# Output products of the two mixers: half of the columns by seven products for three of eight row pairs

## The chip, the cores and the metric

The kernel runs on one core of a Trainium2 chip. The core has a matrix engine (TensorE, PE in the profile, with its weight loads listed as PEld), a vector engine (DVE), a scalar engine (ACT), GpSimd (POOL) and a queue engine that issues most transfers (SP). The metric is the device time of one execution in microseconds; lower is better. All numbers are those of one core.

## The reference

Two layers over 256 tokens of width 2048, in float32. Each layer normalises, mixes tokens, adds, normalises, runs a SwiGLU feed-forward net (FFN) of width 5632, and adds. Layer 0 mixes with an mLSTM, layer 1 with an RG-LRU. Both mixers end in a product with a 2048 by 2048 matrix, and this is where the change lies:

```python
h = h + mlstm_mixer(rms_norm(h, norm_mix[0]), ...)     # ends in  (h_tilde * sigmoid(o)) @ m_w_out
h = h + swiglu(rms_norm(h, norm_ffn[0]), ...)
h = h + rglru_mixer(rms_norm(h, norm_mix[1]), ...)     # ends in  (gelu(gate) * scan) @ r_w_out
h = h + swiglu(rms_norm(h, norm_ffn[1]), ...)
out = rms_norm(h, norm_final)
```

## The kernel before

Weights are read once, in tiles of two 128-row blocks by 512 columns (`raw`, 512 KB each). Every float32 factor is split into a high part, rounded to the PE's reduced type (`whi`, a cast on ACT), and the rest (`wlo`, a subtraction on DVE), and a product is three matmuls: high by high, high by low, low by high. The activations are the stationary operand, in blocks of 128 rows by 128 tokens; the weights move, 512 columns at a time. One accumulator fills one of the eight PSUM banks.

Two routines make products with tokens in the rows. `linear_tok` takes one group of 512 columns (a "quarter" of 2048) and goes through the 16 row blocks k, with two accumulators (the two blocks of 128 tokens). Its weights come through `stream`, whose casts and splits are given a high priority, so that a scheduler, which sets each engine's order when the program is built, puts them ahead of other work. `project_out` calls it once per quarter, adds the result to the residual `h`, and puts the next norm's transposes for that quarter into a list (`later`) that is worked off between matmul groups (`run_pending`).

`paired` takes two groups of 512 columns at once and goes through the row blocks two by two, so that a "row pair" is a 2 by 2 block product: two row blocks by two column groups, for two token blocks. A plain row pair takes eight block products of three matmuls. A row pair that is listed in `seven` takes seven, by Winograd's form of Strassen's scheme: from the four weight tiles of 128 by 512 it makes four differences in place, in the two `raw` tiles, and splits them into four tiles, called s, u, v and t in the code (s, v and t hold 1024 columns, u 512), and the stationary operands include four sums and differences of activation blocks ("forms", s1 to s4). The products go into banks 1 to 8 in the order s, s, u, v, v, t, t; after the last seven pair `mid` adds up banks 1, 5, 6 and 7 (`sums`) so that four banks are free again. Splits in `paired` have no raised priority. The FFN uses it for all of its products.

The tiles `raw`, `whi` and `wlo` come from pools of four buffers, handed out as they are released. The FFN's own pool lends two more of each:

```python
if more[0] and turns[tag] % 6 > 3:
    return more[0].tile([P, 2, NB], dt, tag=tag, name=name, bufs=2)
return wpool.tile([P, 2, NB], dt, tag=tag, name=name)
```

In the mixers `more[0]` is empty, and there are four.

In the mLSTM, four steps j each compute v and o with `linear_tok`, then `turn_y` transposes the gated output `y` and splits it into two of the 16 row blocks (`yh`, `yl`). In the RG-LRU, `gates`, `gelu_branch` and `combine` make a group of four row blocks (`zh`, `zl`); the last group's GELU product (`gb`) is the last PE work before the output product `po`.

Of the kernel before, what the change touches and what calls it, by code (L numbers as in the profile page):

```python
# [38 lines left out]
def kernel(  # L39
# [426 lines left out]


# [14 lines left out]
    def mlstm_mixer():  # L482
        with tc.tile_pool(name="mx", bufs=2) as mx:
# [149 lines left out]
            def turn_y(j, i, y, hi, lo):  # L633
                pt = misc(f"ty{j}{i}").rearrange("p (f t) -> p f t", f=2)
                for f in range(2):
                    for b in range(NT):
                        nc.tensor.transpose(
                            pt[:, f, b * P:(b + 1) * P], y[:, b, (2 * i + f) * P:(2 * i + f + 1) * P], ident
                        )
                for f in range(2):  # L640
                    g = par["g_head"][:, 4 * j + 2 * i + f:4 * j + 2 * i + f + 1]
                    nc.scalar.activation(hi[:, 2 * i + f, :], pt[:, f, :], AF.Copy, scale=g)
# [39 lines left out]
    def ffn(layer, n, nxt):  # L682
        with tc.tile_pool(name=f"ff{layer}", bufs=1) as fp:
            more[0] = fp
            turns.update(raw=-1, whi=-1, wlo=-1)
# [3 lines left out]
            part = {}  # L689

            def sums(bank):

                ea = fp.tile([P, 2, NB], F32, tag="ea", name="ea")
                eb = fp.tile([P, 2, NB], F32, tag="eb", name="eb")
                nc.scalar.copy(ea[:, 0, :], bank[1])
                nc.vector.tensor_tensor(ea[:, 1, :], bank[6], ea[:, 0, :], op=ALU.add)
                nc.vector.tensor_tensor(eb[:, 0, :], bank[7], ea[:, 1, :], op=ALU.add)
                nc.vector.tensor_tensor(ea[:, 1, :], bank[5], ea[:, 1, :], op=ALU.add)
                nc.vector.tensor_tensor(eb[:, 1, :], bank[5], eb[:, 0, :], op=ALU.add)
                part["e"] = ea, eb  # L700

# [32 lines left out]

            def add_out(q, wc, np_, seven, form, last=None):
                def mid(bank):
                    sums(bank)
                    for b, e in enumerate(part["e"]):
                        hs = h[:, b, q * NB:(q + 2) * NB]
                        nc.vector.tensor_tensor(hs, hs, e.rearrange("p s n -> p (s n)"), op=ALU.add)  # L740

                if last:
                    order = [p for p in range(np_) if p not in (np_ - 3, np_ - 1)] + [np_ - 3, np_ - 1]
                    bank = paired(wc, (q * NB, (q + 1) * NB), np_, seven, form, f"po{q}", mid, order, 2)
                    for b, i in enumerate(((2, 3), (4, 8))):
                        last.store(b, [bank[k] for k in i])
                    return
                bank = paired(wc, (q * NB, (q + 1) * NB), np_, seven, form, f"po{q}", mid)
                for i, b, s in ((2, 0, 0), (4, 1, 0), (3, 0, 1), (8, 1, 1)):
                    hs = h[:, b, (q + s) * NB:(q + s + 1) * NB]  # L750
                    nc.vector.tensor_tensor(hs, bank[i], hs, op=ALU.add)
# [47 lines left out]
    def rglru_mixer():  # L799
        with tc.tile_pool(name="rg", bufs=1) as rg:  # L800
# [80 lines left out]
            def combine(j):  # L881
                ge, hs = ges[j], hss[j]
                nc.vector.tensor_tensor(ge, ge, hs, op=ALU.mult)
# [94 lines left out]
```

## Time and profile before

| | us |
|---|---|
| median of three runs (2095.2 to 2096.41) | 2096.27 |
| the profiled execution | 2097.5 |
| its span, first to last instruction | 2095.7 |
| PE busy, DVE busy, ACT busy | 2079.8, 1782.5, 1186.8 |
| mLSTM's output product on PE, first to last matmul's start | 308.4 to 398.9 |
| RG-LRU's output product on PE | 1299.2 to 1388.7 |

In the tables, `out<-in` are the program's names for what an instruction writes and reads; `p` are the FFN's first products and `po` all output products. Idle time is that before an instruction, with what ended it. Busy PE time is modelled, since matmuls overlap; the step from one matmul's start to the next is what counts. Line numbers in the profile are those of the kernel before; the changed kernel's are two higher in the helpers (L447 becomes L449), and further off behind them.

### The profile page before, as it was taken

To read this page: it belongs to the slowest core of one execution; us is meant where nothing else is said; L and a number is where in the kernel's file an instruction comes from. 1 tells how busy PE (TensorE), PEld (TensorE's weight loads), DVE (VectorE), ACT (ScalarE), POOL (GpSimd) and SP (SyncE) were. 2 spreads that over 40 slices of the span, in tenths; PEclk is the share of its full clock that TensorE was granted. 3 is DMA by queue.
4 is the path that set the end of the run, shared out by engine and by line. 5 is a ranking of instruction groups with operands and counts; after the bars stand their busy time and mean duration, and the time that the engine had idled before them with its cause. 6 is when DMAs were issued, how large, how long until landed. Compare 5 with 4: busy or idle time off the path is not lost.

```text
span 2095.7 us, 27022 instructions
## 1 busy us (share of the span) xinstructions
PE 2079.8 (99%) x9794; PEld 1736.4 (83%) x9794; DVE 1782.5 (85%) x2260; ACT 1186.8 (57%) x1529; POOL 40.6 (2%) x60
## 2 busy tenths in 40 slices
PE   9999999999999999999999999999999999999997
PEld 7888888888888888888888888888888888888886
DVE  6755555699999999999997888679999999999998
ACT  5444445556565555565656778556555555555554
POOL 0011110000000000000000000000000000000010
PEclk9999999999999999999999999999999999999999
DMA  7556666666555666665656666666655666656564
GB/s 216 171 161 181 181 181 181 197 205 209 194 201 183 206 213 201 198 203 199 197 189 172 190 190 184 190 200 194 219 183 189 201 205 202 205 197 224 191 201 141
DMA packets 211375, 405.73 MB, mean 194 GB/s; under 512 B 14552, under 2 KB 14760, under 8 KB 211112
## 3 DMA queue, kind: packets, MB, share of 16 engines
q1 hardware_dynamic: 210520, 401.89, 60.0%
q10 hardware_dynamic: 720, 2.10, 0.3%
q8 instruction: 77, 1.26, 0.2%
q14 instruction: 58, 0.48, 0.1%
HBM read 401.84 MB, written 2.10 MB: 193 GB/s over the span
## 4 chain that ended last, share of the span: by engine, by line
PE 96%; DVE 2%; DMA 1%; issue 1%; ACT 0%; POOL 0%; POOLq 0%; SPq 0%; ACTq 0%; DVEq 0%
PE p L384 15%; PE p L386 15%; PE p L385 15%; PE po L385 7%; PE po L386 7%; PE po L384 7%; PE gb L231 3%; PE rec L231 3%; PE po L207 3%; PE po L206 3%; PE po L205 3%; PE qk L231 2%; PE gb L234 1%; PE rec L234 1%; PE v L205 1%; PE v L207 1%
## 5 line engine op out<-in xcount | busy, mean ns | idle before, releaser
L446 ACT CAST whi<-raw 128x1024 fp32r<-128x1024 f32 (+1 forms) x732 | 689.8, 991 | 590.3 <-DVE raw L399 346.0
L447 DVE TENSOR_TENSOR wlo<-raw,whi 128x1024 fp32r<-128x1024 f32 (+1 forms) x732 | 807.8, 1150 | 72.2 <-ACT whi L446 68.8
L384 PE MATMUL p<-whi,z_f 128*128 128x512 f32 x1342 | 523.9, 390 | 0.0
L386 PE MATMUL p<-whi,z_f 128*128 128x512 f32 x1342 | 522.2, 389 | 0.0
L385 PE MATMUL p<-wlo,z_f 128*128 128x512 f32 x1342 | 522.2, 389 | 0.0
L177 DVE TENSOR_TENSOR wlo<-raw,whi 128x1024 fp32r<-128x1024 f32 (+1 forms) x225 | 273.6, 1218 | 172.9 <-ACT whi L175 172.7
L175 ACT CAST whi<-raw 128x1024 fp32r<-128x1024 f32 (+1 forms) x225 | 235.6, 1049 | 209.8 <-PE po L207 64.4
L386 PEld LDWEIGHTS p<-whi,z_f 128*128 128x128 f32 x1342 | 251.9, 188 | 52.5
L384 PEld LDWEIGHTS p<-whi,z_f 128*128 128x128 f32 x1342 | 251.9, 188 | 52.1 <-DVE h L447 0.5
L385 PEld LDWEIGHTS p<-wlo,z_f 128*128 128x128 f32 x1342 | 252.0, 188 | 51.6
L385 PE MATMUL po<-wlo,h 128*128 128x512 f32 x668 | 260.5, 390 | 1.6 <-DVE wlo L447 1.6
L386 PE MATMUL po<-whi,h 128*128 128x512 f32 x668 | 260.0, 389 | 0.0
L384 PE MATMUL po<-whi,h 128*128 128x512 f32 x668 | 259.3, 390 | 0.0
L385 PEld LDWEIGHTS po<-wlo,h 128*128 128x128 f32 x668 | 125.4, 188 | 29.2 <-DVE wlo L447 3.5
L386 PEld LDWEIGHTS po<-whi,h 128*128 128x128 f32 x668 | 125.4, 188 | 25.9
L384 PEld LDWEIGHTS po<-whi,h 128*128 128x128 f32 x668 | 125.3, 188 | 26.0 <-ACT whi L446 0.2
L231 PE MATMUL qk<-x_m,whi 128*128 128x512 f32 x256 | 81.1, 399 | 0.0
L231 PE MATMUL rec<-x_m,whi 128*128 128x512 f32 x256 | 80.5, 396 | 0.0
L231 PE MATMUL gb<-x_m,whi 128*128 128x512 f32 x256 | 80.4, 395 | 0.0
L399 DVE TENSOR_TENSOR raw<-raw,raw 128x512 f32<-128x512 f32 x102 | 70.6, 692 | 3.4
L401 DVE TENSOR_TENSOR raw<-raw,raw 128x512 f32<-128x512 f32 x102 | 70.6, 692 | 3.4
L398 DVE TENSOR_TENSOR raw<-raw 128x512 f32<-128x512 f32 x102 | 70.5, 691 | 3.3
(255 smaller groups left out, 2470.8 us busy)
## 6 DMA issues: line engine op xcount, KB each, us to landing
raw<-in_ffn_w_in_dram SPq DMA_DIRECT2D x352, 512.0 KB, 4.8
raw<-in_ffn_w_out_dram SPq DMA_DIRECT2D x176, 512.0 KB, 5.4
raw<-in_m_w_in_dram SPq DMA_DIRECT2D x95, 512.0 KB, 3.7
raw<-in_r_w_in_dram SPq DMA_DIRECT2D x64, 512.0 KB, 3.9
raw<-in_m_w_out_dram SPq DMA_DIRECT2D x32, 512.0 KB, 3.7
raw<-in_r_w_out_dram SPq DMA_DIRECT2D x32, 512.0 KB, 4.2
gr<-in_r_gate_w_dram SPq DMA_DIRECT2D x8, 512.0 KB, 3.6
h<-in_x_dram SPq DMA_DIRECT2D x4, 512.0 KB, 8.0
```

The costliest lines, as they stand in the source:

```text
L175: cast = nc.scalar.copy(hi[:, at, 0:ncols], r)
L177: nc.vector.tensor_tensor(lo[:, at, 0:ncols], r, hi[:, at, 0:ncols].bitcast(F32), op=ALU.subtract)
L205: nc.tensor.matmul(o, lhsT=ah[:, bs], rhs=hi, start=(k == 0), stop=False)
L207: nc.tensor.matmul(o, lhsT=al[:, bs], rhs=hi, start=False, stop=(k == nk - 1))
L231: nc.tensor.matmul(ps[f], lhsT=hi[:, f * P:(f + 1) * P], rhs=act2(k), start=(k == 0), stop=False, skip_group_check=True)
L384: nc.tensor.matmul(o, lhsT=ah, rhs=bh, start=i not in begun, stop=False)
L385: nc.tensor.matmul(o, lhsT=ah, rhs=bl, start=False, stop=False)
L386: nc.tensor.matmul(o, lhsT=al, rhs=bh, start=False, stop=stop and p == end[i])
L399: nc.vector.tensor_tensor(rb[:, 1, :], rb[:, 1, :], ra[:, 0, :], op=ALU.add)
L401: nc.vector.tensor_tensor(ra[:, 1, :], ra[:, 1, :], rb[:, 1, :], op=ALU.subtract)
L446: nc.scalar.copy(dst_hi, src)
L447: nc.vector.tensor_tensor(dst_lo, src, dst_hi.bitcast(F32), op=ALU.subtract)
```

## The change

In both mixers the first two quarters become one `paired` call over eight row pairs, with seven products in pairs 2, 4 and 6; quarters 2 and 3 go through `project_out` as before. The forms for these three pairs are made where the mixer's output is split. `sums` and `add_out` move out of the FFN unchanged.

```diff
+SEVEN_M = (2, 4, 6)
+SEVEN_R = (2, 4, 6)
...
+    def mixer_out(w, ys, ss, seven, nxt):
+        def form(p, name):
+            if name[0] == "s":
+                return tuple(v[:, int(name[1]) - 1, :] for v in ss[p])
+            f, b = 2 * (p % 2) + int(name[2]) - 1, int(name[1]) - 1
+            return tuple(v[:, f, b * P:(b + 1) * P] for v in ys[p // 2])
+
+        add_out(0, w, NK // 2, seven, form)
+        for q in range(2):
+            later(lambda q=q: nxt.done(q), 4.0)
+        project_out(w, NK, lambda k: tuple(v[:, k % 4, :] for v in ys[k // 4]), nxt, (2, 3))
+
+    def mixer_forms(t, s):
+        f = scratch["forms"]()
+        for o, a, b, neg in ((0, t[1], t[3], True), (1, f[:, 0, :], t[0], True), (2, t[0], t[1], False),
+                             (3, t[2], f[:, 1, :], False)):
+            if neg:
+                nc.vector.scalar_tensor_tensor(out=f[:, o, :], in0=a, scalar=-1.0, in1=b, op0=ALU.mult, op1=ALU.subtract)
+            else:
+                nc.vector.tensor_tensor(f[:, o, :], a, b, op=ALU.subtract)
+        split_store(s[:, 0], s[:, 1], f)
+        return s[:, 0], s[:, 1]
...
@@ turn_y
+                if 2 * j + i in SEVEN_M:
+                    t = scratch["get"]().rearrange("p (s t) -> p s t", t=P)
+                    for f in range(2):
+                        nc.scalar.activation(
+                            t[:, 2 * f:2 * f + 2, :].rearrange("p s t -> p (s t)"), pt[:, f, :], AF.Copy, scale=gs[f]
+                        )
+                    split_store(*(v[:, 2 * i:2 * i + 2, :].rearrange("p f (b t) -> p (f b) t", t=P) for v in (hi, lo)),
+                                t[:, 0:4, :])
...
+                    ss[2 * j + i] = mixer_forms([t[:, n, :] for n in range(4)], sm[-1][:, at % 2])
+                    return
...
@@ mlstm_mixer
-            project_out(m_w_out[0], NK, lambda k: (yh[k // 4][:, k % 4, :], yl[k // 4][:, k % 4, :]), n1)
+            mixer_out(m_w_out[0], ys, ss, SEVEN_M, n1)
...
@@ combine
-                split_store(hi, lo, ge)
+                split_store(*ys[j], ge)
+                for i in range(2):
+                    if 2 * j + i in SEVEN_R:
+                        scratch["forms"] = lambda: rg.tile([P, 4, P], F32, tag="a2", name="forms")
+                        ss[2 * j + i] = mixer_forms(
+                            [ge[:, 2 * i + n // 2, n % 2 * P:(n % 2 + 1) * P] for n in range(4)],
+                            rg.tile([P, 2, 4, P], F32R, tag="rc" if len(ss) < 2 else "hs", name="ss", bufs=2),
+                        )
...
@@ rglru_mixer
-            project_out(r_w_out[0], NK, lambda k: (yh[k // 4][:, k % 4, :], yl[k // 4][:, k % 4, :]), n3)
+            mixer_out(r_w_out[0], ys, ss, SEVEN_R, n3)
```

What this does to the engines' orders is seen at two places; the rest of the program stands as it did. First, DVE at the start of the RG-LRU's output product. Before, the gathers of the last GELU product (L242), its norm factor (L877), its product with the scan (L883) and the split into `zl` (L447) stand between splits of weights (`wlo`, L177):

```order
L242 TENSOR_TENSOR ge_11302<-gb_2_11124,ge_11302 128x256
L177 TENSOR_TENSOR wlo_11411<-raw_11408,whi_11410 128x1024
L242 TENSOR_TENSOR ge_11302<-gb_3_11125,ge_11302 128x256
L877 TENSOR_TENSOR ge_11302<-ge_11302,rbc_m_9364 128x1024
L177 TENSOR_TENSOR wlo_11429<-raw_11426,whi_11428 128x1024
L883 TENSOR_TENSOR ge_11302<-ge_11302,hs_11117 128x1024
L177 TENSOR_TENSOR wlo_11447<-raw_11444,whi_11446 128x1024
L447 TENSOR_TENSOR zl_9257<-ge_11302,zh_9256 128x1024
L177 TENSOR_TENSOR wlo_11469<-raw_11466,whi_11468 128x1024
```

Now, from pair 2's second difference (L400) to its third and fourth splits (`wlo_11487` and `wlo_11489`, from L449), the product with the scan (L927), pair 6's forms (L519, L521) and `zl` come in between:

```order
L927 TENSOR_TENSOR ge_11380<-ge_11380,hs_11195 128x1024
L401 TENSOR_TENSOR raw_11480<-raw_11480,raw_11478 128x512
L519 SCALAR_TENSOR_TENSOR forms<-ge_11380 128x128
L521 TENSOR_TENSOR forms<-ge_11380 128x128
L519 SCALAR_TENSOR_TENSOR forms<-forms,ge_11380 128x128
L449 TENSOR_TENSOR zl_9319<-ge_11380,zh_9318 128x1024
L521 TENSOR_TENSOR forms<-ge_11380,forms 128x128
L449 TENSOR_TENSOR wlo_11487<-raw_11480,whi_11486 128x1024
L449 TENSOR_TENSOR ss<-forms,ss 128x512
L403 TENSOR_TENSOR raw_11478<-raw_11478,raw_11480 128x512
L449 TENSOR_TENSOR wlo_11489<-raw_11478,whi_11488 128x1024
```

The last group's gate and GELU work, which stood among splits of later rows, now stands ahead of two splits of row pair 2.

Second, DVE at the first addition into `h` in the mLSTM's output product. Before, a quarter's two additions (L440) stand among splits, and the norm's transposes follow a quarter later on PE:

```order
L177 TENSOR_TENSOR wlo_2850<-raw_2847,whi_2849 128x1024
L177 TENSOR_TENSOR wlo_2891<-raw_2888,whi_2890 128x1024
L440 TENSOR_TENSOR h<-po_0_2661,h 128x512
L440 TENSOR_TENSOR h<-po_1_2662,h 128x512
L177 TENSOR_TENSOR wlo_2909<-raw_2906,whi_2908 128x1024
```

Now the sums of banks 5, 6 and 7 (`e`), the additions of these sums (L487) and those of banks 2, 4, 3 and 8 (L498) come, with the splits of quarter 2 between them:

```order
L179 TENSOR_TENSOR wlo_3129<-raw_3126,whi_3128 128x1024
L478 TENSOR_TENSOR e<-po_5_2820,e 128x512
L487 TENSOR_TENSOR h<-h,e 128x1024
L179 TENSOR_TENSOR wlo_3147<-raw_3144,whi_3146 128x1024
L487 TENSOR_TENSOR h<-h,e 128x1024
L179 TENSOR_TENSOR wlo_3165<-raw_3162,whi_3164 128x1024
L498 TENSOR_TENSOR h<-po_2_2684,h 128x512
L498 TENSOR_TENSOR h<-po_4_2691,h 128x512
L498 TENSOR_TENSOR h<-po_3_2702,h 128x512
L179 TENSOR_TENSOR wlo_3183<-raw_3180,whi_3182 128x1024
L498 TENSOR_TENSOR h<-po_8_2709,h 128x512
```

Both quarters of `h` become complete together, and on PE their transposes (`tr_f`) stand within the third pair of quarter 2's row blocks:

```order
L207 MATMUL po_1_3038<-whi_3128,yh_170 128x512
L208 MATMUL po_1_3038<-wlo_3129,yh_170 128x512
L344 MATMUL tr_f_3070<-ident,h 128x128 x3
L344 MATMUL tr_f_3079<-ident,h 128x128 x3
L344 MATMUL tr_f_3099<-ident,h 128x128
L344 MATMUL tr_f_3113<-ident,h 128x128
L209 MATMUL po_1_3038<-whi_3128,yl_171 128x512
```

More of the change, by code (lines that the diff above doesn't have):

```diff
@@ L465, in log1p_exp_nabs_half, with sums, add_out, mid @@
         return p
+    part = {}
+    def sums(bank):
+        ea, eb = scratch["sums"]()
+        nc.scalar.copy(ea[:, 0, :], bank[1])
+        nc.vector.tensor_tensor(ea[:, 1, :], bank[6], ea[:, 0, :], op=ALU.add)
+        nc.vector.tensor_tensor(eb[:, 0, :], bank[7], ea[:, 1, :], op=ALU.add)
+        nc.vector.tensor_tensor(ea[:, 1, :], bank[5], ea[:, 1, :], op=ALU.add)
+        nc.vector.tensor_tensor(eb[:, 1, :], bank[5], eb[:, 0, :], op=ALU.add)
+        part["e"] = ea, eb
+    def add_out(q, w, n, seven, form, last=None):
+        def mid(bank):
+            sums(bank)
+            for b, e in enumerate(part["e"]):
+                hs = h[:, b, q * NB:(q + 2) * NB]
+                nc.vector.tensor_tensor(hs, hs, e.rearrange("p s n -> p (s n)"), op=ALU.add)
+        if last:
+            order = [p for p in range(n) if p not in (n - 3, n - 1)] + [n - 3, n - 1]
+            bank = paired(w, (q * NB, (q + 1) * NB), n, seven, form, f"po{q}", mid, order, 2)
+            for b, i in enumerate(((2, 3), (4, 8))):
+                last.store(b, [bank[k] for k in i])
+            return
+        bank = paired(w, (q * NB, (q + 1) * NB), n, seven, form, f"po{q}", mid)
+        for i, b, s in ((2, 0, 0), (4, 1, 0), (3, 0, 1), (8, 1, 1)):
+            hs = h[:, b, (q + s) * NB:(q + s + 1) * NB]
+            nc.vector.tensor_tensor(hs, bank[i], hs, op=ALU.add)
@@ L639, in turn_y @@
                         )
+                gs = [par["g_head"][:, 4 * j + 2 * i + f:4 * j + 2 * i + f + 1] for f in range(2)]
+                if 2 * j + i in SEVEN_M:
[6 more added lines that the diff above has]
+                                t[:, 0:4, :])
+                    scratch["forms"] = lambda: t[:, 4:8, :]
+                    at = len(ss)
+                    if at % 2 == 0:
+                        sm.append(mx.tile([P, 2 - at // 2, 2, 4, P], F32R, tag=("kT", "prs0")[at // 2], name="ss", bufs=1))
+                    ss[2 * j + i] = mixer_forms([t[:, n, :] for n in range(4)], sm[-1][:, at % 2])
+                    return
                 for f in range(2):
-                    g = par["g_head"][:, 4 * j + 2 * i + f:4 * j + 2 * i + f + 1]
-                    nc.scalar.activation(hi[:, 2 * i + f, :], pt[:, f, :], AF.Copy, scale=g)
+                    nc.scalar.activation(hi[:, 2 * i + f, :], pt[:, f, :], AF.Copy, scale=gs[f])
                 for f in range(2):
-                    g = par["g_head"][:, 4 * j + 2 * i + f:4 * j + 2 * i + f + 1]
                     nc.vector.scalar_tensor_tensor(
-                        out=lo[:, 2 * i + f, :], in0=pt[:, f, :], scalar=g,
+                        out=lo[:, 2 * i + f, :], in0=pt[:, f, :], scalar=gs[f],
                         in1=hi[:, 2 * i + f, :].bitcast(F32), op0=ALU.mult, op1=ALU.subtract,
                     )
-            yh, yl = [], []
+            ss, sm = {}, []
             for j in range(4):
@@ L672, in mlstm_mixer, with two @@
                 hi, lo = ys[j]
-                yh.append(hi)
-                yl.append(lo)
                 for i in range(2):
                     later(lambda i=i, y=y, hi=hi, lo=lo, j=j: turn_y(j, i, y, hi, lo))
-            project_out(m_w_out[0], NK, lambda k: (yh[k // 4][:, k % 4, :], yl[k // 4][:, k % 4, :]), n1)
+            def two():
+                e = mx.tile([P, 2, 2, NB], F32, tag="qT", name="e", bufs=1)
+                return e[:, 0], e[:, 1]
+            scratch["sums"] = two
+            mixer_out(m_w_out[0], ys, ss, SEVEN_M, n1)
     mlstm_mixer()
@@ L684, in ffn @@
             more[0] = fp
+            scratch["sums"] = lambda: [fp.tile([P, 2, NB], F32, tag=t, name=t) for t in ("ea", "eb")]
             turns.update(raw=-1, whi=-1, wlo=-1)
@@ L688, in ffn @@
             made = []
[L689 to L700, printed above, removed]
             def turn(j, i, hid, e):
@@ L733, in group @@
                 later(lambda: [turn(j, i, hid, (ea, eb)) for i in range(2)], 8.0)
[L735 to L751, printed above, removed]
             for c0, c1 in CHUNKS:
@@ L805, in rglru_mixer @@
             gwv = r_gate_w[0].rearrange("g (k p) o -> p (g k) o", p=P)
-            yh, yl = {}, {}
+            ss = {}
             rvs, rvhs, rvls, ges, hss = {}, {}, {}, {}, {}
@@ L896, in rglru_mixer @@
                     recurrent(j + 2)
-            project_out(r_w_out[0], NK, lambda k: (yh[k // 4][:, k % 4, :], yl[k // 4][:, k % 4, :]), n3)
+            scratch["sums"] = lambda: [rg.tile([P, 2, NB], F32, tag="rvh", name="e", bufs=2) for _ in range(2)]
+            mixer_out(r_w_out[0], ys, ss, SEVEN_R, n3)
     rglru_mixer()
```

3 lines of the change are left out of this document (removed).

## The prediction

> **What bounds the kernel.** I read the page first (busy times and chain), then PE's waits, then a table of stretches.
>
> ```profile
> span 2095.7 us, 27022 instructions
> PE 2079.8 (99%) x9794; PEld 1736.4 (83%) x9794; DVE 1782.5 (85%) x2260; ACT 1186.8 (57%) x1529; POOL 40.6 (2%) x60
> ...
> PE 96%; DVE 2%; DMA 1%; issue 1%; ACT 0%; POOL 0%; POOLq 0%; SPq 0%; ACTq 0%; DVEq 0%
> ```
> ```profile
> PE po L385 <- DVE wlo L447: 1.6, 2, 0.8
> ```
> ```profile
> 0.00:50.00 50.00, 45.45 (x261) 37.97 (x262) 31.68 (x68) 30.28 (x60) 3.06 (x13) 1.00 0.73 224
> ...
> 300.00:350.00 50.00, 50.00 (x230) 41.50 (x229) 27.09 (x31) 24.77 (x32) 0.00 (x0) 1.00 0.62 186
> ...
> 500.00:550.00 50.00, 50.00 (x226) 41.51 (x225) 47.53 (x59) 28.38 (x34) 0.00 (x0) 1.00 0.54 180
> ...
> 1250.00:1300.00 50.00, 50.00 (x303) 44.32 (x302) 40.08 (x49) 45.88 (x65) 0.00 (x0) 1.00 0.63 190
> ...
> 2050.00:2100.00 50.00, 35.75 (x156) 28.62 (x154) 37.40 (x53) 21.20 (x33) 1.10 (x2) 0.93 0.36 126
> ```
>
> PE is the bound from end to end: 96% of the chain, and in all FFN and mixer products only 1.6 us of waiting. So a matmul that goes saves its whole interval, and any wait that comes is paid in full. The columns of the table after the stretch and its length are busy PE, PE loads, DVE, ACT, POOL, then clock, DMA share and GB/s. The mLSTM output products (300 to 350) leave DVE 23 us idle of 50; the FFN, which already uses seven products, leaves it 2.5.
>
> **Term A, the matmuls.** First and last of 46 matmuls in a row of the RG-LRU output product:
>
> ```profile
> 1299.18 0.40 PE L205 MATMUL po<-whi,zh 128*128 128x512 f32 x1
> ...
> 1309.39 0.39 PE L205 MATMUL po<-whi,zh 128*128 128x512 f32 x1
> ```
>
> 10.21 us over 45 steps is 0.227 us each. A row pair of 512 by 512 weights costs 24 matmuls (5.45 us) plain and 21 (4.77 us) with seven products. Three pairs in two mixers save 18 matmuls: **4.1 us**, which is 0.195%. That is all there is to win.
>
> **What is added.** Per mixer, forms of three activation pairs (four 128-wide operations, a 512-wide cast and a 512-wide low half each) and, per seven pair, a third 1024-wide split, a 512-wide one and four 512-wide differences where two 1024-wide splits stood.
>
> ```profile
> L447 DVE TENSOR_TENSOR wlo<-raw,whi 128x1024 fp32r<-128x1024 f32 x630 | 743.5, 1224 | 72.2 <-ACT whi L446 68.8
> L446 ACT CAST whi<-raw 128x1024 fp32r<-128x1024 f32 x630 | 634.3, 1052 | 578.7 <-DVE raw L399 346.0 <-PE p L386 89.5 <-PE po L386 60.2
> ...
> L399 DVE TENSOR_TENSOR raw<-raw,raw 128x512 f32<-128x512 f32 x102 | 70.6, 692 | 3.4
> ...
> L446 ACT CAST whi<-raw 128x512 fp32r<-128x512 f32 x102 | 62.7, 615 | 11.6 <-PE po L386 9.9 <-ACT whi L446 1.6
> ...
> L330 DVE TENSOR_TENSOR zh<-zh 128x128 f32<-128x128 f32 x36 | 10.2, 284 | 0.0
> ...
> L642 ACT ACTIVATE yh<-ty,cols 128x256 fp32r<-128x256 f32 x16 | 6.7, 469 | 3.2 <-PE ty L637 3.2
> ```
> DVE, then ACT, in the FFN's output product, where this path runs today:
> ```profile
> 714.51 1.22 DVE L740 TENSOR_TENSOR h<-h,ea 128x1024 f32<-128x1024 f32 x1
> 715.64 1.22 DVE L740 TENSOR_TENSOR h<-h,eb 128x1024 f32<-128x1024 f32 x1
> 716.78 2.48 DVE L751 TENSOR_TENSOR h<-po,h 128x512 f32<-128x512 f32 x4
> ...
> 722.04 0.68 DVE L397 TENSOR_TENSOR raw<-raw,raw 128x512 f32<-128x512 f32 x1
> 722.76 0.69 DVE L398 TENSOR_TENSOR raw<-raw 128x512 f32<-128x512 f32 x1
> 723.49 0.69 DVE L399 TENSOR_TENSOR raw<-raw,raw 128x512 f32<-128x512 f32 x1
> ```
> ```profile
> 724.50 3.90 ACT L446 CAST whi<-raw 128x1024 fp32r<-128x1024 f32 x4 [7.54 <-PE po L386]
> ```
>
> Back to back, DVE starts a 1024-wide operation every 1.13 us and a 512-wide one every 0.60 (2.48 less 0.68, over 3); where one needs the one before it, 0.72. ACT starts the cast 0.3 us after DVE's third difference ends (723.49 + 0.69 to 724.50). A seven pair thus takes DVE 3 x 1.13 + 0.60 + 4 x 0.72 = 6.9 us where a plain one takes 2.3, in 4.77 us of PE. Forms for pairs 2 and 4 are made while v, o and gb products run; I cost them at nothing, under DVE's 23 idle us, though ACT at 1250 to 1300 has only 4 us left, so the 512-wide cast (0.6 us) may push what follows there. The transposes of y, the norm's transposes and the DMA count stay as they were.
>
> **Term B, the RG-LRU mixer's entry.** Gate arithmetic and GELU of the last quarter come on DVE when po begins at 1299.18. Today they end late and harm nobody, since weight splits go ahead of them and their result is needed by k = 12 only:
>
> ```profile
> 1296.55 1.06 ACT L865 ACTIVATE th<-th 128x1024 f32<-128x1024 f32 x1
> ```
> ```profile
> 1297.64 1.23 DVE L866 SCALAR_TENSOR_TENSOR th<-th,ii 128x1024 f32<-128x1024 f32 x1 [0.95 <-ACT th L865]
> ...
> 1302.19 1.27 DVE L870 TENSOR_TENSOR_SCAN hs<-r,th 128x256 f32<-128x256 f32 x2
> ...
> 1305.68 1.06 DVE L242 TENSOR_TENSOR ge<-gb,ge 128x256 f32<-128x256 f32 x3
> ...
> 1311.02 1.23 DVE L883 TENSOR_TENSOR ge<-ge,hs 128x1024 f32<-128x1024 f32 x1 [0.42 <-ACT ge L878]
> ```
>
> In the new order they, and the forms of pair 6, stand on DVE ahead of pair 2's third and fourth splits. From L866 (waiting for the root on ACT, so no earlier) to pair 2's last low half I count ten 1024-wide operations (11.3), four scans at 0.6 (2.4), four gathers (1.06 for three: 1.4), six 512-wide at 0.6 to 0.72 (4.0), four forms (1.1): 20.2 us without a pause. One pause is sure: the last cast waits for the last difference (0.3 + 1.05 us), with nothing else queued. So the split is done 20.2 + 1.4 us after 1297.64, that is 20.0 us after po begins. PE wants it after two plain pairs and 18 matmuls, 10.9 + 4.1 = 15.0 us. **Wait 5.1 us**, in pieces under 2 us (first for the third split's cast, then its low half, then the fourth's). Bounds: 3.7 without the pause, 5.7 with ACT 0.6 us late.
>
> **Term C, raw buffers.** The FFN's pools lend two more buffers of each kind; the mixers have four, and a row pair takes two raw ones. So pair 4 loads into pair 2's two, pair 6 into pair 4's, and these are free only when DVE has made the last splits. Landing of the mixers' loads, mLSTM's and RG-LRU's:
>
> ```profile
> DMA to landing us min/median/max: 3.6/4.0/6.2
> ```
> ```profile
> DMA to landing us min/median/max: 3.5/4.3/6.7
> ```
>
> One turn from third split to third split: issue 0.1, landing 4.0, cast 1.05, splits 1.13 + 0.6, three differences 2.16, hand-over 0.3, cast 1.05, split 1.22: 11.6 us. PE's turn is 5.45 + 4.77 = 10.2, so each turn loses 1.4 us once slack is gone. In the mLSTM mixer pair 2's third split is ready about 2 us before its matmul (transposes of y after pair 0 at 5.5 us, then ACT's two 0.47 and two 0.6, the third split's 1.05 + 1.22, and about 2 us for transposes, hand-overs and the buffer that pair 1 frees: 11.8, wanted at 13.9), so pair 4 is covered and pair 6 waits about 1.0. In RG-LRU pair 2 is late already; pairs 4 and 6 wait 1.1 each. **3.2 us**; with landings of 3.6 about 0.5, with 6.2 to 6.7 about 10. I take the medians, since pair 4's two loads are let go 1.1 us apart (third split, then fourth) and DMA is at 0.62 of its time in this stage.
>
> **Term D, the exit.** The norm's transposes of quarters 0 and 1 stand on PE 27 (mLSTM) and 32 matmuls into quarter 2 and need all of h's additions. On DVE, from pair 6's last split to the first finished block of h, stand seven 1024-wide splits (7.9), four sums (2.6), two 1024-wide additions (2.4) and one 512-wide (0.6): 13.5 us, plus a wait of up to 1 us for a buffer that PE frees late. PE arrives after 56 or 61 matmuls, 12.7 or 13.8 us, and the last block of h follows one split and three additions later. I take 1.2 + 0.8 = **2.0 us**; 0 to 4 as the buffer wait falls. Queued behind PE's wait are quarter 2's matmuls, so it is paid. Quarter 2's first two loads go past nothing new on SP, but use pair 6's raw buffers: free some 8 us before PE needs their splits, against 4.0 for landing and 2.3 for a split, so I cost them at nothing; landing at 6.5, they would cost about 0.7. POOL's moved memset is under its 98% of idle time.
>
> **Sum.** -4.1 + 5.1 + 3.2 + 2.0 = +6.2 us. The profiled execution took 2097.5 us (span 2095.7), 1.2 above the median 2096.27: profiled span near 2102, median **2102.5 us**. All low ends give 2096.4, all high ends 2112.
>
> **Rivals.**
> (1) Not slower. Averages decide: a mixer's added DVE work is 3 x 4.6 + 3 x 1.9 = 19.5 us against 40 idle us in its 90 us of output products. That needs pair 2's last split within 15.0 us of po's start, so DVE would have to reach the chain at 1297.64 some 5 us earlier; ACT's root there speaks against it. Time 2092.2, or 2094 with half of D.
> (2) Only the entry waits: landings near 3.6 and a free buffer at the exit hide C and D: 2096.27 - 4.1 + 5.1 = 2097.3.
> (3) Loads land late, near 6.5 us, because pairs of them leave together: C rises to 10, time 2109.
> (4) The waits slow PE's clock. After the last matmul the clock falls: 0.93 over the 45.7 us that are left in the last stretch is some 6.4 us at half. One such stretch within the mixer costs 3.2 us: 2105.7; two, 2109. Against it: PE waited 4.5 us in its first 50 and the clock there is 1.00. The Trainium skill (TensorE: Matmul & The Clock Gate, Part 1) says that the clock halves after an idle window of about 3.4 us; by that rule gaps under 2 us between matmuls cost nothing more, and the trace agrees as far as it goes.
>
> **Chances.** The forecast (2099.5 to 2105.5) 0.52, (1) 0.15, (2) 0.13, (3) 0.12, (4) 0.08. What a measurement of this kernel can tell from no change is about 0.2%, 4.2 us. Term A alone stays within that, so faster has 0.02; (1), (2) and the lower end of the forecast make 0.29 for the same; slower 0.69. The range leaves out (1) and the upper ends of (3) and (4): 2096.5 to 2109.
>
> **What would show it.** PE's waits should name L387 and L386 of po on wlo and whi, about 10 us in all, the largest part within 25 us of RG-LRU's po. DVE should be busy without a pause there. The norm's transposes should wait for h once or twice per mixer. PE's matmuls must be 18 fewer. If PE shows no wait on po, B is wrong and (1) holds; if the mLSTM mixer waits more than RG-LRU, C is mis-sized.

## Result, and the profile after

The changed kernel takes 2106.39 us (median of four, 2103.69 to 2108.98) against 2095.87 for the kernel before (median of four): a ratio of 1.0048, 95% interval 1.0036 to 1.006, or 10.5 us slower. The profiled execution took 2103.69 us, the lowest of the four.

From the page, span and busy times:

```profile
span 2101.9 us, 27100 instructions
PE 2080.4 (99%) x9776; PEld 1734.0 (82%) x9776; DVE 1824.4 (87%) x2335; ACT 1198.8 (57%) x1552; POOL 40.6 (2%) x60
```

PE has 18 matmuls fewer (9794 before), and DVE 41.9 us more work. From the table of waits, PE's own on `po` and `tr_f` (total us, how often, the longest):

```profile
PE po L387 <- DVE wlo L449: 3.5, 5, 0.9
PE po L386 <- ACT whi L448: 3.0, 4, 1.3
PE tr_f L344 <- DVE h L498: 2.9, 2, 2.0
```

Two of the five waits in the first row, 1.6 us together, stand in the FFN and were there before. The mixers have thus 1.9 + 3.0 + 2.9 = 7.8 us of new waits. Their places are in PE's timeline (start, length, then in brackets the idle time before the instruction and what ended it); the first two lines are from the mLSTM's output product, the others from the RG-LRU's, which begins at 1298.82:

```profile
342.26 0.50 PE L387 MATMUL po<-wlo,ss 128*128 128x512 f32 x1 [0.76 <-DVE wlo L449]
...
358.59 0.44 PE L344 MATMUL tr_f<-ident,h 128*128 128x128 f32 x2 [1.96 <-DVE h L498]
```
```profile
1313.22 0.73 PE L386 MATMUL po<-whi,ss 128*128 128x512 f32 x2 [1.28 <-ACT whi L448]
1314.87 0.50 PE L387 MATMUL po<-wlo,ss 128*128 128x512 f32 x1 [0.92 <-DVE wlo L449]
...
1317.23 0.80 PE L386 MATMUL po<-whi,ss 128*128 128x512 f32 x1 [1.16 <-ACT whi L448]
...
1328.39 0.50 PE L387 MATMUL po<-wlo,ss 128*128 128x512 f32 x1 [0.22 <-DVE wlo L449]
...
1339.06 0.73 PE L386 MATMUL po<-whi,ss 128*128 128x512 f32 x2 [0.34 <-ACT whi L448]
1340.02 0.50 PE L386 MATMUL po<-whi,ss 128*128 128x512 f32 x1 [0.22 <-ACT whi L448]
...
1356.42 0.44 PE L344 MATMUL tr_f<-ident,h 128*128 128x128 f32 x2 [0.93 <-DVE h L498]
```

The first three lines of the RG-LRU are its pair 2 (third split's cast, its low half, fourth split's cast), then come pair 4, pair 6 and the exit, where the next norm's transposes wait for `h`. A table of stretches around them (busy PE, PE loads, DVE, ACT, POOL, then granted clock, DMA share, GB/s), first of the kernel before, then of the one after:

```profile
1310.00:1320.00 10.00, 10.00 (x46) 8.28 (x45) 6.97 (x7) 6.03 (x6) 0.00 (x0) 1.00 0.66 201
```
```profile
1310.00:1315.00 5.00, 2.79 (x12) 1.68 (x11) 5.00 (x10) 2.61 (x3) 0.00 (x0) 1.00 0.00 0
1315.00:1320.00 5.00, 3.84 (x10) 2.62 (x11) 3.81 (x5) 3.17 (x4) 0.00 (x0) 0.71 0.44 113
1320.00:1325.00 5.00, 5.00 (x22) 4.07 (x21) 3.70 (x5) 1.45 (x2) 0.00 (x0) 0.95 0.86 294
```

DVE is busy without a pause from 1310 to 1315 while PE starves, and no transfer runs. Then the clock falls: 0.71 and 0.95 are 5 x 0.29 x 2 + 5 x 0.05 x 2 = 3.4 us at half rate, right behind the waits.

How long each mixer's output product lasts is read off PE's timeline, from the first `po` to the next norm's first `p`; the RG-LRU's before begins at 1299.18 (shown above) and gives 1388.93 - 1299.18 = 89.75 us, the one after 1395.47 - 1298.82 = 96.65:

```profile
1388.93 0.39 PE L384 MATMUL p<-whi,z_f 128*128 128x512 f32 x1
```
```profile
1298.82 0.40 PE L386 MATMUL po<-whi,zh 128*128 128x512 f32 x1
...
1395.47 0.39 PE L386 MATMUL p<-whi,z_f 128*128 128x512 f32 x1
```

The table has these stages for every kernel of this study, with the medians. "By stages" is the median of the kernel before in the groups of the experiments, 2095.7, plus what the two stages of the profile have gained or lost; it differs from the median where the profiled execution or the rest of the program does.

| kernel | mLSTM's stage | RG-LRU's stage | by stages | median (runs) |
|---|---|---|---|---|
| before | 90.68 | 89.75 | | 2095.7 |
| after | 92.38 | 96.65 | 2104.3 | 2106.39 (4) |
| e1_mlstm | 94.08 | 89.75 | 2099.1 | 2098.89 (11) |
| e2_rglru | 90.73 | 97.48 | 2103.5 | 2103.56 (5) |
| e3_exit | 90.36 | 95.26 | 2100.9 | 2101.67 (6) |
| e4_two | 95.07 | 91.29 | 2101.6 | 2101.30 (7) |
| e5_ahead | 92.80 | 95.00 | 2103.1 | 2101.19 (5) |
| e6_raw | 90.33 | 93.11 | 2098.7 | 2099.81 (11) |
| e7_warm | 90.68 | 95.58 | 2101.5 | 2102.37 (6) |
| e8_turn | 88.70 | 94.01 | 2098.0 | 2097.84 (11) |
| e9_first | 88.70 | 90.91 | 2094.9 | 2094.69 (11) |
| e10_both | 88.69 | 91.30 | 2095.3 | 2096.05 (11) |
| e11_mlstm_turn | 88.72 | 89.75 | 2093.7 | 2095.23 (11) |
| e12_two | 88.70 | 88.51 | 2092.5 | 2092.47 (11) |

In a stage without waits the seven products would give 9 x 0.227 = 2.04 us: 88.64 and 87.71.

### The profile page after: what moved, and what is told of

Its sections match the earlier page's. It is cut to its first block, busy times and chain, and to the rows that moved or that the text cites. A ratio compares the mean times of both kernels' runs of the same rounds, so it can differ in the third digit from the quotient of the medians.

```text
span 2101.9 us, 27100 instructions
## 1 busy us (share of the span) xinstructions
PE 2080.4 (99%) x9776; PEld 1734.0 (82%) x9776; DVE 1824.4 (87%) x2335; ACT 1198.8 (57%) x1552; POOL 40.6 (2%) x60
## 3 DMA queue, kind: packets, MB, share of 16 engines
q8 instruction: 76, 1.25, 0.2%
## 4 chain that ended last, share of the span: by engine, by line
PE 91%; DVE 4%; DMA 2%; ACT 2%; issue 1%; POOL 0%; POOLq 0%; ACTq 0%; SPq 0%; DVEq 0%
PE p L388 14%; PE p L386 14%; PE p L387 14%; PE po L387 7%; PE po L388 7%; PE po L386 7%; PE rec L233 3%; PE gb L233 2%; PE qk L233 2%; DVE wlo L449 1%; PE rec L236 1%; PE v L207 1%; PE v L208 1%; PE v L209 1%; PE o L209 1%; PE o L207 1%
## 5 line engine op out<-in xcount | busy, mean ns | idle before, releaser
L449 DVE TENSOR_TENSOR wlo<-raw,whi 128x1024 fp32r<-128x1024 f32 (+1 forms) x776 | 857.6, 1151 | 91.0 <-ACT whi L448 87.5
L177 ACT CAST whi<-raw 128x1024 fp32r<-128x1024 f32 (+1 forms) x193 | 201.8, 1048 | 165.2 <-PE v L209 36.2
L403 DVE TENSOR_TENSOR raw<-raw,raw 128x512 f32<-128x512 f32 x108 | 74.8, 692 | 3.6
L401 DVE TENSOR_TENSOR raw<-raw,raw 128x512 f32<-128x512 f32 x108 | 74.7, 692 | 3.6
L400 DVE TENSOR_TENSOR raw<-raw 128x512 f32<-128x512 f32 x108 | 74.6, 691 | 3.5
```

Of the source, the lines that this page charges most:

```text
L177: cast = nc.scalar.copy(hi[:, at, 0:ncols], r)
L400: nc.vector.tensor_tensor(rb[:, 0, :], rb[:, 1, :], rb[:, 0, :], op=ALU.subtract)
L401: nc.vector.tensor_tensor(rb[:, 1, :], rb[:, 1, :], ra[:, 0, :], op=ALU.add)
L403: nc.vector.tensor_tensor(ra[:, 1, :], ra[:, 1, :], rb[:, 1, :], op=ALU.subtract)
L449: nc.vector.tensor_tensor(dst_lo, src, dst_hi.bitcast(F32), op=ALU.subtract)
```

## The experiments

The kernels of each group below ran together on one chip, with the kernel before among them; e11_mlstm_turn and e12_two are a group of their own. The kernel before has medians of 2095.65 to 2095.73 us in the four groups.

### One mixer at a time, the exit, and one pair fewer

**e1_mlstm**: the change in the mLSTM alone.

```diff
-SEVEN_R = (2, 4, 6)
+SEVEN_R = ()
-            mixer_out(r_w_out[0], ys, ss, SEVEN_R, n3)
+            project_out(r_w_out[0], NK, lambda k: tuple(v[:, k % 4, :] for v in ys[k // 4]), n3)
```

> The change in the mLSTM alone; the RG-LRU's output product as it was before. Main theory (most of the loss is the RG-LRU's entry, where the gate and GELU work stands on DVE ahead of pair 2's splits): between the two stages' starts the profile of the changed kernel lost 1.7 us in the mLSTM, so 2097.6 (2096.5 to 2098.5), no stretch with a lower PE clock before the end, PE waits on po about 0.8 us and on the norm's transposes about 2.0. Rival (the paired path with four buffers costs the same wherever it stands): half of the 10.5 us, 2101.

2098.89 us, ratio 1.0015 (1.0006 to 1.0023): 3.2 us slower, 0.4 us above the theory's range and well under the rival's 2101. The theory wanted no stretch of lower clock; beside pair 6's wait (0.76 us) and 2.0 us of the exit, the profile has one at half clock, behind the exit's wait (0.94 from 350 to 360, 0.89 from 360 to 370: 3.4 us at half).

**e2_rglru**: the change in the RG-LRU alone, by the same two lines for the mLSTM.

> The change in the RG-LRU alone; the mLSTM's output product as it was before. Main theory: 6.9 us in the profile of the changed kernel, plus up to 2 us where the waits lower PE's clock more than once: 2103 to 2105, with three waits of 1 us or more in the first 20 us of po. Rival (the same cost in both mixers): 2101.

2103.56 us, ratio 1.0034 (1.0021 to 1.0046): 7.9 us slower, as the theory said, though two of its three waits are under 1 us (1.27, 0.92 and 0.63). The two alone add up to 3.2 + 7.9 = 11.1, against 10.5 for both: within the scatter of the runs the mixers' losses simply add.

**e3_exit**: the changed kernel, with the norm's transposes of quarters 0 and 1 put off by 8 us of PE's work.

```diff
-            later(lambda q=q: nxt.done(q), 4.0)
+            later(lambda q=q: nxt.done(q), 12.0)
```

> Both mixers changed; the norm's transposes of quarters 0 and 1 are put 8 us later into quarter 2 (12.0 for 4.0). If the additions into h are merely late for them (term D): PE's waits on tr_f, 2.9 us in the changed kernel, go, and 2106.4 becomes 2103.5. If DVE has too much to do there altogether: the wait turns up at the matmuls of quarter 2 or 3 instead, 2106.

2101.67 us, ratio 1.0031 (1.0019 to 1.0044): 4.5 us less than the change costs (6.0 over its before in place of 10.5), and 1.8 under the 2103.5 expected. No wait on `tr_f` is left in either mixer. The stages are 2.0 and 1.4 us shorter; the rest, about 1 us, is in the difference between the profiled executions and the medians, where stretches at half clock like that of e1_mlstm may come and go; that is not shown.

**e4_two**: RG-LRU's pair 2 by eight products again.

```diff
-SEVEN_R = (2, 4, 6)
+SEVEN_R = (4, 6)
```

> Both mixers changed, but in the RG-LRU only pairs 4 and 6 take seven products; pair 2 is plain (3 matmuls more, 0.7 us). Main theory (pair 2's splits are late): the 5.8 us lost up to pair 4's start go, lowered clock included, and what is left in the RG-LRU are pair 6's wait and the exit: 2106.4 - 5.8 - 1 (further stretches of lower clock in the runs) + 0.7 = 2100.3 (2098.5 to 2101.5). Rival (raw buffers and the exit make the loss): 2105 or more.

2101.30 us, ratio 1.0026 (1.0015 to 1.0037), a little over what was expected and far from the rival. RG-LRU's entry has no wait left:

```profile
1310.00:1320.00 10.00, 10.00 (x45) 8.27 (x45) 10.00 (x14) 6.09 (x7) 0.00 (x0) 1.00 0.81 262
1320.00:1330.00 10.00, 10.00 (x46) 8.26 (x44) 8.23 (x9) 5.16 (x5) 0.00 (x0) 1.00 0.37 103
```

One pair of seven at this place costs 96.65 - 91.29 = 5.4 us net, or 6.0 without the 0.7 us that its three matmuls save; and it is rather more, since RG-LRU's exit waits 1.91 us here and 0.93 in the changed kernel. DVE is still busy throughout from 1310 to 1320: there is no room for more.

### Order, buffers and clock

The three of this group all have e3_exit's edit.

**e5_ahead**: the splits of RG-LRU's pairs 0, 1 and 2 ahead on DVE and ACT.

```diff
+                with tc.high_priority(offset=AHEAD) if p in ahead else nullcontext():
                     split_store(sh, sl, ra)
 ...
+            mixer_out(r_w_out[0], ys, ss, SEVEN_R, n3, ahead=(0, 1, 2))
```

> The changed kernel with the exit's norm put off (as e3_exit) and, in RG-LRU's paired quarters, the splits of pairs 0, 1 and 2 given priority, so that on VectorE they stand ahead of the last gate product, of GELU's evacuation and of the last forms. Nothing else is changed. Theory (VectorE's queue at the entry is what pair 2 waits for): the three waits of the entry, 1.26 + 0.92 + 1.16 us in e3_exit's trace and the half clock of some 1.7 us behind them go, RG-LRU's output stage is 90.0 us long (95.26 in e3_exit), the time 2101.7 - 5 = 2096.5, between 2095 and 2098. Rival (the entry is held by the loads or by ScalarE's halves, not by VectorE's order): the waits stay over 2 us in sum and the time is above 2099.5. Second rival (the forms come late in place of the splits): the waits move to pairs 4 and 6, the stage is 92 to 94 us, the time 2098.5 to 2100.5.

2101.19 us, ratio 1.0032 (1.0019 to 1.0044): nothing gained over e3_exit; the first theory's 2096.5 is a miss. The second rival has the place right, with a longer wait than it gave. Pair 2 does not wait any more, but pair 4 does:

```profile
1328.00 1.74 PE L386 MATMUL po<-whi,ss 128*128 128x512 f32 x3 [3.30 <-ACT whi L450]
```

The reason is seen on ACT, in the order of its queue: a cast of pair 3's raw tile waits for its transfer, and behind it stand GELU's table load and GELU. On DVE the last forms need GELU's result, and pair 4's differences stand behind them:

```profile
1317.03 1.05 ACT L450 CAST whi<-raw 128x1024 fp32r<-128x1024 f32 x1 [1.60 <-DMA raw<-in_r_w_out_dram]
1318.10 1.28 ACT L924 ACT_TABLE_LOAD   x1
1319.39 1.06 ACT L924 ACTIVATE ge<-ge 128x1024 f32<-128x1024 f32 x1
```

**e6_raw**: e5_ahead with two more raw buffers in the RG-LRU, in the tiles `rvl`, dead by then.

```diff
-            return more[0].tile([P, 2, NB], dt, tag=tag, name=name, bufs=2)
+            return more[0].tile([P, 2, NB], dt, tag=dead[0] or tag, name=name, bufs=2)
 ...
+            more[0], dead[0] = rg, "rvl"
+            turns.update(raw=-1)
             mixer_out(r_w_out[0], ys, ss, SEVEN_R, n3, ahead=(0, 1, 2))
+            more[0] = dead[0] = None
```

> e5_ahead, and two more raw buffers for RG-LRU's paired quarters, in the place of two tiles that are dead by then (rvl), so that the loads of a pair can land while the raw tiles of the pair before are still being combined. If the turn of the raw buffers costs what the prediction gave it (1.1 us at each of RG-LRU's pairs 4 and 6), the waits at pairs 4 and 6 go and the time is 1.5 to 2.2 us under e5_ahead's. If not, the two are within 0.5 us.

2099.81 us, ratio 1.002 (1.0011 to 1.0028): 1.4 us under e5_ahead, where at least 1.5 was expected. The intervals of the two overlap, but the RG-LRU's stage is 1.9 us shorter: the wait of 3.30 becomes 2.09, pair 6's go. What is left is DVE's own time, which now has hardly a pause (10.00, 10.00 and 9.31 of each 10 us):

```profile
1300.00:1310.00 10.00, 9.96 (x44) 7.97 (x43) 10.00 (x15) 4.22 (x7) 0.00 (x0) 1.00 0.22 71
1310.00:1320.00 10.00, 9.91 (x43) 7.80 (x42) 10.00 (x14) 7.07 (x8) 0.00 (x0) 1.00 0.66 210
1320.00:1330.00 10.00, 7.69 (x26) 5.57 (x25) 9.31 (x12) 6.10 (x7) 0.00 (x0) 0.83 0.31 97
```

**e7_warm**: e3_exit with 16 matmuls that no one reads, in the places where PE waits in pair 2.

```diff
+            if p == 2 and scratch.get("warm") and nm == "s3":
+                warm(form(p, "s4")[0], sh[:, 0, :], 3)
 ...
+            for _ in range(k):
+                nc.tensor.matmul(bank[5], lhsT=a, rhs=b, start=True, stop=True, skip_group_check=True)
 ...
+                    if p == 2 and scratch.get("warm") and nm in ("s3", "s1"):
+                        warm(form(p, "s4")[0], sh[:, 0, :], 5 if nm == "s3" else 8)
```

> e3_exit, and 16 more matmuls of 128x512 in RG-LRU's pair 2, six ahead of the third split's first product, five ahead of its low half's, five ahead of the fourth split's; they use operands that are there already and write a bank that is begun afresh afterwards, so they change no value. They take 16 x 0.227 = 3.6 us, where TensorE waited 1.26 + 0.92 + 1.16 us and the pipeline's refilling with it. Theory (the half clock behind the entry comes from the three waits close together): with the waits filled the granted clock is 1.00 in 1310 to 1325 us, the stage is 1.7 us shorter than e3_exit's where that one had its stretch at half clock, and the time 2100.2, between 2099 and 2101.3, with a smaller spread. Rival (the clock falls for another reason, or on its own): the clock falls below 0.95 in this window all the same, and the time is 2101.7 to 2103.

The same stretches, of e3_exit and then of e7_warm:

```profile
1308.00:1316.00 8.00, 4.66 (x18) 2.77 (x16) 6.81 (x12) 4.21 (x5) 0.00 (x0) 0.99 0.06 7
1316.00:1320.00 4.00, 4.00 (x12) 2.92 (x11) 3.86 (x4) 2.39 (x3) 0.00 (x0) 0.60 0.85 243
```
```profile
1308.00:1316.00 8.00, 8.00 (x35) 6.23 (x34) 7.39 (x13) 3.09 (x4) 0.00 (x0) 1.00 0.03 11
1316.00:1320.00 4.00, 3.79 (x15) 2.46 (x14) 3.39 (x3) 3.23 (x4) 0.00 (x0) 1.00 0.67 178
```

As far as the clock goes, the theory holds: with the waits filled it stays at 1.00. The time does not follow: 2102.37 us, ratio 1.0034 (1.0021 to 1.0046), not 2100.2, and no better than e3_exit. Entry and pair 2 came out 1.2 us shorter than in e3_exit; then pair 4 waited 0.20 + 0.76 us for its splits, where e3_exit had no wait. What the half clock had covered is time that pair 4's splits needed anyway.

That is the common thread. PE's first product with a form of pair 6 starts this long after RG-LRU's first `po`: 39.0 us in the changed kernel, 39.2 in e2_rglru, 38.7 in e3_exit, 39.0 in e7_warm, 38.9 in e5_ahead. Without waits it would be 144 matmuls, 32.7 us. These five differ in where PE waits, in the order of the splits and in the clock, and they are late by 6.0 to 6.5 us all the same. What the changed kernel and e7_warm share is seen on DVE (first the lines of the changed kernel, then those of e7_warm, whose `po` begins at 1298.23):

```profile
1317.21 3.50 DVE L449 TENSOR_TENSOR wlo<-raw,whi 128x1024 fp32r<-128x1024 f32 x3 [1.19 <-ACT whi L448]
...
1323.23 0.69 DVE L399 TENSOR_TENSOR raw<-raw,raw 128x512 f32<-128x512 f32 x1 [1.15 <-DMA raw<-in_r_w_out_dram]
```
```profile
1316.61 3.50 DVE L459 TENSOR_TENSOR wlo<-raw,whi 128x1024 fp32r<-128x1024 f32 x3 [1.19 <-ACT whi L458]
...
1322.63 0.69 DVE L407 TENSOR_TENSOR raw<-raw,raw 128x512 f32<-128x512 f32 x1 [1.08 <-DMA raw<-in_r_w_out_dram]
```

Counted from the first `po`, DVE begins the last split of pair 2 after 18.39 and 18.38 us, and pair 4's first difference, which waits for the transfer of its raw tile, after 24.41 and 24.40. What PE does meanwhile changes neither. So DVE owes work (a debt, below) up to pair 2's splits, and behind them stands the turn of the raw buffers, since pair 4 loads into pair 2's. In e6_raw, with two more buffers, pair 6 begins after 37.9 us. In e8_turn (below), which lends buffers in another way, it is 38.8: PE has no wait there behind the entry, but its clock is at half for 6.8 us, and no run tells what it would be at full clock.

### Repairs

These kernels too have e3_exit's edit.

**e8_turn**: two more raw buffers for pairs 3 and 6 of both mixers, in tiles of the last norm's output; no priority.

```diff
+        if more_raw:
+            spare[0] = True
+            turns["raw"] = -3
 ...
+        if spare[0] and tag == "raw" and turns[tag] > 0 and turns[tag] % 6 > 3:
+            return xpool.tile([P, 2, NB], dt, tag=f"x{turns[tag] % 6 - 2}", name=name)
```

> e3_exit with two more raw buffers for pairs 3 and 6 of both mixers' paired quarters, in the place of tiles of the last norm's output that are dead by then; no instruction is given priority and the order of pairs is the changed kernel's. Theory (pair 6 waits since its raw tiles come late through the turn of four buffers; e3_exit's trace has 0.34 + 0.76 us there in the mLSTM and 0.43 + 0.21 in RG-LRU): these four waits go, the entry's three stay, the time is 1.2 to 1.7 us under e3_exit's 2101.7, so 2100.2. Rival (pair 6 waits for VectorE's own time in its four subtractions and splits, not for the loads): the waits stay within 0.3 us of what they were and the time is within 0.6 us of e3_exit's.

2097.84 us, ratio 1.0009 (1.0 to 1.0018): 3.8 us under e3_exit, more than expected. The mLSTM's stage is 88.70 us, with no wait left: the seven products bring their full 2.0 us there. In the RG-LRU pair 6's waits go and the entry's stay, the third of them at 0.28 us:

```profile
1309.42 0.74 PE L388 MATMUL po<-whi,ss 128*128 128x512 f32 x2 [1.27 <-ACT whi L452]
1311.08 0.80 PE L389 MATMUL po<-wlo,ss 128*128 128x512 f32 x1 [0.92 <-DVE wlo L453]
1313.44 0.79 PE L388 MATMUL po<-whi,ss 128*128 128x512 f32 x1 [0.28 <-ACT whi L452]
```

**e9_first**: e8_turn with another order of pairs in the RG-LRU, FIRST = (0, 1, 3, 2, 5, 4, 6, 7).

```diff
-            mixer_out(r_w_out[0], ys, ss, SEVEN_R, n3, more_raw=True)
+            mixer_out(r_w_out[0], ys, ss, SEVEN_R, n3, FIRST, more_raw=True)
```

> e8_turn with RG-LRU's pairs in the order 0, 1, 3, 2, 5, 4, 6, 7, so that a pair with eight products stands between the entry and the first pair with seven. No instruction is given priority. Theory (at the entry VectorE has more to do than TensorE's first pairs take, gate, GELU and forms with 6.7 us of splits for a pair of seven; 5.4 us more of TensorE's work ahead of it cover that): the entry's waits of 3.3 us and their half clock go, and pair 6, right behind pair 4, gets up to 2 us of wait; RG-LRU's output stage is 88 to 91 us, the time 2096 (2094.5 to 2098). Rival (what VectorE owes only moves on, as in e5_ahead, where 3.3 us came back at pair 4): 3 us or more of wait in pairs 2, 4 and 6, the time 2099 to 2101.

2094.69 us, ratio 0.9996 (0.9987 to 1.0004), as the theory said. RG-LRU's stage is 90.91 us, 3.1 less than in e8_turn, and the clock stays at 1.00. What is left stands in pair 2 and, larger, in pair 6 right behind pair 4:

```profile
1315.37 0.73 PE L388 MATMUL po<-whi,ss 128*128 128x512 f32 x2 [0.38 <-ACT whi L452]
1316.31 0.50 PE L388 MATMUL po<-whi,ss 128*128 128x512 f32 x1 [0.22 <-ACT whi L452]
1332.30 0.73 PE L388 MATMUL po<-whi,ss 128*128 128x512 f32 x2 [1.08 <-ACT whi L452]
1333.26 0.50 PE L388 MATMUL po<-whi,ss 128*128 128x512 f32 x1 [0.22 <-ACT whi L452]
```

**e10_both**: e9_first, with priority for the splits of RG-LRU's pairs 0, 1, 3, 2 and for the last GELU.

```diff
-            mixer_out(r_w_out[0], ys, ss, SEVEN_R, n3, FIRST, more_raw=True)
+            mixer_out(r_w_out[0], ys, ss, SEVEN_R, n3, FIRST, ahead=(0, 1, 3, 2), more_raw=True)
 ...
-                nc.scalar.activation(ge, ge, AF.Gelu_apprx_tanh)
+                with tc.high_priority(offset=2 * AHEAD) if j == 3 else nullcontext():
+                    nc.scalar.activation(ge, ge, AF.Gelu_apprx_tanh)
```

> e9_first, and the splits of RG-LRU's pairs 0, 1, 3 and 2 and the last GELU are given priority: pair 2's splits stand ahead of the last forms, and GELU stands on ScalarE behind the first split of pair 2. Theory: as e9_first, with what is left of pair 2's wait gone: 0 to 1 us under e9_first, between 2094 and 2097.5. Rival (the forms of pair 6 or VectorE's load at pairs 4 and 6 take it back): within 0.5 us of e9_first or slower than it.

2096.05 us, ratio 1.0003 (0.9994 to 1.0012), 1.4 us over e9_first: the rival, though the two intervals overlap and the RG-LRU's stage is only 0.4 us longer. Pair 2 waits 0.60 us, as before in sum, and pair 6 1.35 + 0.21, 0.26 more. Order alone pays nothing off.

**e11_mlstm_turn**: the change in the mLSTM alone (by e1_mlstm's two lines), with e8_turn's buffers.

> The change in the mLSTM alone (RG-LRU's four quarters as before), with the exit's norm put off and two more raw buffers for pairs 3 and 6 as in e8_turn. Theory (the products are worth 9 x 0.227 = 2.0 us, and the exit and the turn of buffers were all that took them back): 2095.7 - 2.0 = 2093.7, between 2093.0 and 2094.6, under the kernel before in nearly every run. Rival (e8_turn's short mLSTM stage of 88.7 us is a matter of one profile, and something else gives the 2 us back after it): 2095 or more.

2095.23 us, ratio 0.9996 (0.9987 to 1.0005); 2093.7 was expected, and the forecast range is missed, though a ratio of 0.9991, which that would be, lies within the interval. The mLSTM's stage is 88.72 us, so the 2.0 us are there, and the rival's "after it" is wrong for the profiled execution: most of its loss lies ahead of the stage, whose first `po` begins at 309.54 us, against 306.22 in e8_turn with the same mLSTM. In the first 60 us, which the edits leave alone, PE waits 1.90 us for the first norm's scale, and the clock is 0.94 from 30 to 60, 3.6 us at half:

```profile
37.28 0.67 PE L319 MATMUL bc_m<-dg_m,ones 128*128 128x256 f32 x2 [1.90 <-DVE dg_m L317]
```

That was the slowest execution of eleven (2097.25 us; the fastest was 2093.44). Whether the others lost their 1 to 2 us in the same way can't be said from one profile; it stays open. In the fourteen profiles of this study the first `po` begins between 306.12 and 309.56 us, so up to 3.4 us of any difference between two executions can come from ahead of the stages.

**e12_two**: e9_first with RG-LRU's pair 6 by eight products.

```diff
-SEVEN_R = (2, 4, 6)
+SEVEN_R = (2, 4)
```

> e9_first with RG-LRU's pair 6 by eight products, so that its order is eight, eight, eight, seven, eight, seven, eight, eight. Three matmuls of 0.227 us come back, 0.7 us; if pair 6 waits in e9_first because it stands right behind pair 4 (1.08 + 0.22 us, and some 0.3 us of refilling for each wait), 1.3 to 1.9 us go: 2094.7 - 0.9 = 2093.8, between 2093.2 and 2094.5. Rival (the wait moves to pair 4, or goes for another reason): 2095 to 2095.5.

2092.47 us (2091.49 to 2093.84), ratio 0.9985 (0.9976 to 0.9994): 3.2 us under the kernel before, whose fastest run in this group was 2094.66, and 13.9 us under the changed kernel. It is also 0.7 us under the range expected: not only pair 6's waits are gone but pair 2's as well (0.38 + 0.22 us in e9_first), and DVE has no forms of pair 6 to make ahead of pair 2's splits, which may be why. The RG-LRU's stage has no wait at all; PE is busy through the 50 us of which it had 45.84 in the changed kernel:

```profile
1300.00:1350.00 50.00, 45.84 (x188) 35.40 (x187) 43.09 (x54) 25.52 (x28) 0.00 (x0) 0.97 0.48 156
```
```profile
1300.00:1350.00 50.00, 50.00 (x222) 41.32 (x221) 44.47 (x50) 28.38 (x36) 0.00 (x0) 1.00 0.57 186
```

(The first row is the changed kernel's, the second e12_two's.) Fifteen matmuls fewer are 3.4 us; 3.2 were measured. Once nothing waits, a product that is left out saves its time almost in full, and in this order, with these buffers and this exit, DVE has room for five of the six pairs.

## Why the prediction held, point by point

The forecast was slower, 2102.5 us in a range of 2096.5 to 2109; 2106.39 came. The direction and the largest cause were right, the middle was 4 us low, and the time lies above the 2099.5 to 2105.5 that the forecast proper was given. By stages the profiled execution lost 1.70 + 6.90 = 8.6 us where the sum had 6.2; the median lies 1.9 us above that execution's 8.6. Of the signs named, the 18 matmuls, DVE without a pause and one wait of the transposes in each mixer came; the new waits on `po` are 4.9 us, not about 10.

- **Term A, -4.1.** Right: 18 matmuls fewer, and 1.98 us in a mixer without waits (e8_turn's mLSTM, 90.68 to 88.70).
- **Term B, +5.1.** The place, the three pieces and the cause were right: pair 2's last split was foretold done 20.0 us after the first `po`, and DVE ends it after about 19.6. The three waits are 3.36 us; from start to start, with the pipeline's refilling behind each, about 4.1; and 1.7 us come from the clock: 5.8 in all. What the step did not have is that the wait is a debt of DVE, with the turn of the raw buffers behind it, so that about as much comes back when the splits are put first (e5_ahead) or when PE's clock is held (e7_warm); e4_two gives at least 6.0 for one pair of seven at this place. It took room on PE ahead of the pair, 5.4 us (e9_first), to pay it.
- **Term C, +3.2.** Right in size, in part by luck. Pair 6 of the mLSTM waits 0.76 us (1.0 foretold); RG-LRU's pairs 4 and 6 wait 0.22 and 0.56, not 1.1 each, since the longer wait in pair 2 had moved PE back. These waits add up to 1.54 us. Two more buffers shorten the stages by 1.7 and 1.25 us (e3_exit to e8_turn), 2.9 together; but RG-LRU's part also holds a shorter third wait in pair 2 and a second stretch at half clock. The hand-over of 0.3 us was read off a row whose wait PE ended; where DVE ends it, it is 0.1 (e7_warm: 1324.62 + 0.69 to 1325.42).
- **Term D, +2.0.** The term that was mis-sized. The transposes wait 2.0 us in the mLSTM and 0.9 in the RG-LRU, 2.9 for 1.2 + 0.8. Taking the wait away gives 3.4 us in the stages and 4.5 in the medians (e3_exit), which would fit a half clock behind this wait in some executions, as in e1_mlstm; the changed kernel's profile has none there.
- **Rival (4), the clock.** This is the step that failed. Of gaps under 2 us I wrote that they "cost nothing more, and the trace agrees as far as it goes", and gave it 0.08. The clock fell behind pair 2's waits in the changed kernel, none of them over 1.3 us. It gave 3.2 us to a stretch, read off the end of the kernel, where PE has nothing left to do; one costs 1.7, since 3.4 us at half rate do half their work. With four raw buffers in the RG-LRU, a clock that is held gains nothing (e7_warm): pair 4's splits are late in any case. With e8_turn's buffers, and behind the exits, no run holds the clock, so what it costs there is open. The spread of the runs, 2103.69 to 2108.98, would fit up to three such stretches more than in the profiled execution, but that is argued only: no other execution of the changed kernel has a profile.
- **Rivals (1) and (2)** are out for this kernel: it is slower, and besides the entry 1.54 us of buffer waits and 2.9 of the exits stand in its profile. On average DVE has room, and e12_two shows that the averages can be had, with another order, buffers and exit. (With half of term D, rival (1) would be 2093.2, not 2094.) **Rival (3)**: transfers landed in 3.6/4.4/6.3 (mLSTM) and 3.6/4.4/6.1 us (RG-LRU; least, median, most), against 3.6/4.0/6.2 and 3.5/4.3/6.7 before the change, so it is out too.

## What to carry to other kernels

Trading PE's work for DVE's paid here only where DVE had no debt: count, from the stage's own timeline, what DVE must finish by each matmul that needs it, not its idle share over the stage. When a wait goes away and comes back at the next group with about the same size, as in e5_ahead, the queue's order alone is not the cause; put work that the starved engine can do ahead of it, lend buffers to the loads, or take a smaller part of the saving, as e12_two does. An exit's transposes belong where the last additions are surely done: 8 us of delay in one number was worth 4.5 us here.
